# Moving the memory keys, the transposes and half of the memory values in a two-layer decoder trunk

## The chip, the cores and the metric

The kernel runs on one core of one Trainium2 chip. The metric is device time in microseconds (us) of one execution. The engines are named as in the profile: PE is TensorE's matmul, PEld its weight load, DVE is VectorE, ACT is ScalarE, POOL is GpSimd and SP is SyncE, which only issues transfers here.

## The reference

Two layers work on x of 512 tokens by 1024 channels, all in fp32. Each layer has three sub-layers, each followed by LayerNorm(alpha * x + f(x)):

```python
h = hybrid_mixer(x, ...)                 # three mixers, gated and merged, then  merged @ w_out
x = layer_norm(ALPHA * x + h, ln1_g, ln1_b)
x = layer_norm(ALPHA * x + memory_cross_attention(x, mem, xq, xkv, xo), ln2_g, ln2_b)
x = layer_norm(ALPHA * x + swiglu(x, w_up, w_down), ln3_g, ln3_b)

def memory_cross_attention(x, mem, wq, wkv, wo):   # 4 heads of 256, 256 memory tokens
    q = x @ wq;  k, v = split(mem @ wkv, 2)
    p = softmax(q k^T / 16)                        # per head
    return (p @ v) @ wo
```

The memory tokens are the same for both layers. Keys and values depend on them and on the layer's weights alone, so they can be computed at any place ahead of their use; the queries need the rows that the first LayerNorm has finished.

## The kernel before

Each fp32 operand is held as two parts: a high part, rounded to fp32r (the name ends in h), and a low part, the difference (l). A product is three matmuls: high by high, high by low, low by high. Weights come in 372 chunks of 128 x 1024. A chunk is loaded by `load_raw` (L269, on SP's queue), its high part is cast on ACT in `split_chunk` (L277), and its low part is a subtraction issued by `flush` (L284), on DVE, but on POOL for the chunks in `on_pool`: the memory key tiles 2 to 7 and the first two up-projection tile pairs. Chunks are split in the order of their use. Each step has a limit `pairs` on the chunks that are split and not yet used up; `refill` brings at most two new ones per step, and three raw chunks are loaded beyond those split. All buffers of 4 KB a partition (raw and split chunks, activations in transposed form, memory keys and values, query and output parts) come from one pool of 39, tag `a4`.

The order of the work is written out by hand in `make_program` as a list of steps for PE. Step kinds are "a" (an output tile of 128 channels by all tokens, 24 matmuls of 512 columns; for memory keys 256 columns, L828 to L830), "b" (a row tile of 128 tokens by 512 channels, 24 matmuls, L859 to L861) and "k" (all four row tiles of the cross-attention's output projection, for one head's part of the sum, L841 to L843). For each step the main loop calls `refill`, then the `post` function of the step before (the copy out of PSUM), then advances the side work, emits the matmuls, and calls `flush`. Side work is a list of Python generators: the stages of attention heads (`attn_x`, `attn_xv`), LayerNorm rows (`ln_item`) and others. Each `yield` ends a stage; a generator goes on one stage at a step, provided the steps since the last time add up to more than 0.75 (a full tile counts 1, a memory key tile 0.5). Half of the active generators go on ahead of the step's matmuls, the others in their middle. Where a step needs a result that isn't issued yet (`need`), the side work is advanced until it is.

Around the change, each layer goes: merge of the third branch, memory key tiles 0 and 1, output projection `w_out` as row tiles (first half of the channels, four row tiles; then the second half), memory key tiles 2 to 7, the memory values as four row tiles, eight query tiles, four "k" steps of `xo` (first half of the channels), four row tiles of `xo` (second half), and the FFN. `post_ln` adds a row tile to the residual (L697) and takes statistics (L698). After the second half of a row it starts `ln_item`, which normalises the row with two passes on DVE (L496, L499) and a power on POOL between them (L492), then waits some stages (3 for the first LayerNorm), and transposes the row on PE (L512), with copies to high parts on ACT (L518) and low parts on DVE (L519).

For a head of the cross-attention, `attn_x` has three stages for each of four row blocks: scores and exponentials (L444 to L450), scaling by the sum (L453, L454), transposes and split (L458 to L464). With the last block done, `attn_xv` multiplies with the values (L476 to L478) and splits the result (L479, L480) for the "k" step of that head.

Of the kernel before, what the change touches and what calls it, by code (L numbers as in the profile page):

```python
# [56 lines left out]
def make_program():  # L57

    chunks, steps = [], []

    def ch(name, l, k0, nk, c0, nc_):
        chunks.append((name, l, k0, nk, c0, nc_))
        return len(chunks) - 1

    def tile_step(name, l, c0, act, post, n0=0, n1=S, **kw):
        c = ch(name, l, 0, KT, c0, P)
        st = Step("a", [c], act=act, post=post, nk=KT, ncol=P, off=0, n0=n0, n1=n1, **kw)  # L70
        steps.append(st)
        return st

    def group(name, l, k0, nk, c0, act, post, pairs, tokens=NT, needs=None, pre=None):
        cs = [ch(name, l, k0 + 2 * k, 2, c0, 512) for k in range(nk // 2)]
        for t in range(tokens):
            st = Step("b", cs, act=act, post=post + (t,), t=t, pairs=pairs)
            if needs:
                st.need = tuple(n.format(t=t) for n in needs)
            if pre and t == 0:  # L80
                st.pre = pre
            steps.append(st)

    for l in range(L):
        def a_head(h, pairs):
            tile_step("w_in", l, OFF_AQ + P * h, "x", ("rope", l, "A", h, 0), pairs=pairs)
            tile_step("w_in", l, OFF_AK + P * h, "x", ("rope", l, "A", h, 1), pairs=pairs)

        def c_pair(u):
            tile_step("w_in", l, OFF_CQ + P * u, "x", ("rope", l, "C", u, 0))  # L90
            tile_step("w_in", l, OFF_CK + P * u, "x", ("rope", l, "C", u, 1))

        def gates(br, *ns):
            for n in ns:
                tile_step("w_in", l, OFF_GL + {"A": 0, "B": D, "C": 2 * D}[br] + P * n, "x",
                          ("gate", l, br, n))

        def project(br, n):
            c = ch({"A": "w_br_a", "C": "w_br_c"}[br], l, 0, 4, P * n, 2 * P)
            for m in (0, 1):  # L100
                steps.append(Step("a", [c], act="o" + br, post=("merge", l, br, n + m), nk=4,
                                  ncol=2 * P, off=P * m, n0=0, n1=S, need=("o%s%d" % (br, l),)))

        if l == 0:
            a_head(0, 6)
            a_head(1, 6)
            group("w_in", l, 0, KT, OFF_AV, "x", ("v", l, "A"), 6)
            gates("A", 0, 1)
            a_head(2, 4)
            gates("A", 2, 3, 4)  # L110
            a_head(3, 4)
            gates("A", 5, 6, 7)
        else:
            group("w_in", l, 0, KT, OFF_AV, "x", ("v", l, "A"), 6,
                  needs=("x%d_3_{t}" % (l - 1),), pre=("tabs",))
            for h in range(4):
                a_head(h, 5 if h < 2 else 4)
                gates("A", 2 * h, 2 * h + 1)
        group("w_in", l, 0, KT, OFF_CV, "x", ("v", l, "C"), 5)
        c_pair(0)  # L120
        gates("C", 0)
        c_pair(1)
        project("A", 0)
        project("A", 2)
        c_pair(2)
        project("A", 4)
        project("A", 6)
        c_pair(3)
        for n in range(KT):
            st = tile_step("w_in", l, OFF_RX + P * n, "x", ("rx", l, n))  # L130
            if n < 2:
                st.pre = ("gw", l, n)
            tile_step("w_in", l, OFF_RG + P * n, "x", ("rg", l, n))
            if n < KT - 1:
                gates("C", n + 1)
            if n in (3, 4, 5, 7):
                project("C", {3: 0, 4: 2, 5: 4, 7: 6}[n])
        for n in range(KT):
            tile_step("w_in", l, OFF_GL + D + P * n, "x", ("gate", l, "B", n))
        for n in range(KT):  # L140
            tile_step("w_br_b", l, P * n, "oB", ("merge", l, "B", n), need=("oB%d" % l,),
                      pre=("mem", l) if n == 5 else None)
        for kt in range(2):
            tile_step("xkv", l, P * kt, "mem", ("memk", l, kt), n0=0, n1=MEM, pairs=5)
        for h in range(2):
            group("w_out", l, 0, KT, 512 * h, "m", ("ln", l, 1, h), 5,
                  needs=("m%d" % l,))
        for kt in range(2, KT):
            tile_step("xkv", l, P * kt, "mem", ("memk", l, kt), n0=0, n1=MEM, pairs=5)
        for h in range(2):  # L150
            group("xkv", l, 0, KT, D + 512 * h, "mem", ("memv", l, h), 5, tokens=2)
        for kt in range(KT):
            tile_step("xq", l, P * kt, "x", ("xq", l, kt),
                      need=tuple("x%d_1_%d" % (l, t) for t in range(NT)))
        for h in range(4):
            steps.append(Step("k", [ch("xo", l, 2 * h, 2, 0, 512)], act="ox", k0=2 * h,
                              post=("lns", l, 2, 0) if h == 3 else None, pairs=4,
                              need=("ox%d_%d" % (l, h),)))
        group("xo", l, 0, KT, 512, "ox", ("ln", l, 2, 1), 6)
        for gi, (j0, nj) in enumerate(GROUPS):  # L160
            if gi == 0:
                cs = [ch("w_up", l, 0, KT, HID * (i % 2) + P * (i // 2), P) for i in range(4)]
                for hf in range(2):
                    for i in range(4):
                        steps.append(Step(
                            "a", [cs[i]], act="x", nk=KT, ncol=P, off=0,
                            n0=256 * hf, n1=256 * hf + 256, bank="up%d" % i,
                            post=("up", l, i // 2, i % 2) if hf else None, pairs=6,
                            need=("x%d_2_%d" % (l, 2 * hf), "x%d_2_%d" % (l, 2 * hf + 1))))
            for j in range(j0 + (2 if gi == 0 else 0), j0 + nj):  # L170
                tile_step("w_up", l, P * j, "x", ("up", l, j, 0), pairs=6)
                tile_step("w_up", l, HID + P * j, "x", ("up", l, j, 1), pairs=6)
            for h in range(2):
                group("w_down", l, j0, nj, 512 * h, "h",
                      ("ln", l, 3, h) if gi else ("acc", l, h), 7)
    return chunks, steps
# [3 lines left out]
def kernel(  # L180
# [72 lines left out]
    for s, st in enumerate(steps):  # L253
        for c in st.chunks:
            last_use[c] = s
            if first_use[c] is None:
                first_use[c] = s
    on_pool = {c for c, (name, l, k0, nk, c0, n) in enumerate(chunks)
               if (name == "xkv" and 2 * P <= c0 < D) or (name == "w_up" and c0 % HID < 2 * P)}
    raws, hi, lo, late = {}, {}, {}, []  # L260
    ptr = {"raw": 0, "split": 0}
    RAW_AHEAD = 3
# [9 lines left out]
    def split_chunk(s):  # L272
        c = ptr["split"]
        while ptr["raw"] <= c:
            load_raw()
        h, lw, raw = a4("whi", [1024], F32R), a4("wlo", [1024], F32R), raws.pop(c)
        A.copy(h, raw)  # L277
        hi[c], lo[c] = h, lw
        late.append((lw, raw, h, G if c in on_pool else V))
        ptr["split"] += 1  # L280

    def flush():
        for lw, raw, h, eng in late:
            eng.tensor_tensor(lw, raw, f(h), ALU.subtract)  # L284
        late.clear()
        while ptr["raw"] < min(NCH, ptr["split"] + RAW_AHEAD):
            load_raw()
# [20 lines left out]
    for l in range(L):  # L308
        goals["oA%d" % l] = goals["oC%d" % l] = 16
        goals["oB%d" % l] = KT  # L310
        goals["m%d" % l] = KT

    def met(k):
        return done.get(k, 0) >= goals.get(k, 1)
# [152 lines left out]

    def attn_xv(l, h, w):
        wh, wl = w
        acts["ox"].append((a4("oxh", [2, S], F32R), a4("oxl", [2, S], F32R)))  # L470
        oh, ol = acts["ox"][h]
        for k in range(2):
# [6 lines left out]
            A.copy(oh[:, k, :], o)  # L479
            V.tensor_tensor(ol[:, k, :], o, f(oh[:, k, :]), ALU.subtract)  # L480
        mark("ox%d_%d" % (l, h))
        return
        yield

    lnst, lnp = {}, {}

    def ln_item(l, which, t, waits):
# [14 lines left out]
                nc.sync.dma_start(out[t * P:(t + 1) * P, c], xt[:, c])  # L502
        if last:
            return
        for _ in range(waits):
            yield
        if t == 0:
# [182 lines left out]
    def post_ln(ps, l, which, half, t):  # L690
# [6 lines left out]
        V.scalar_tensor_tensor(xs, ps, co, xs, ALU.mult, ALU.add)  # L697
        V.bn_stats(lnst[t][:, 6 * half:6 * half + 6], xs)  # L698
        if half == 1:
            waits = 3 if which == 1 else 2 if t == NT - 1 else 1  # L700
            g = ln_item(l, which, t, waits)
            if step_side(g):
                fresh.append(g)
# [23 lines left out]
    def post_memv(ps, l, half, t):  # L727
        if half == 0 and t == 0:
            acts["mv"] = [(a4("mvh", [1024], F32R), a4("mvl", [1024], F32R)) for _ in range(2)]
        dh, dl = (m[:, 512 * half:512 * half + 512] for m in acts["mv"][t])  # L730
        A.copy(dh, ps)
        V.tensor_tensor(dl, ps, f(dh), ALU.subtract)

    def post_xq(ps, l, kt):
        h = kt // 2
# [348 lines left out]
```

## Time and profile before

| | us |
|---|---|
| median of 3 runs | 2190.14 |
| lowest, highest | 2189.81, 2190.46 |
| the profiled execution | 2190.57 |
| its span, first to last instruction | 2188.5 |

The span is what the trace covers; the execution's time has some 2 us around it. Busy time of an engine is the union of its instructions' durations; an instruction of PE is shown until its modelled end, so that neighbours overlap. In a timeline the columns are start, duration (both us), engine, line, operation, output and inputs by the program's names, shapes and a count of merged instructions; in brackets the idle time of the engine just before and what ended it. The granted clock is the share of TensorE's full speed that was allowed.

### The profile page before, as it was taken

Reading aid. Unit: us, or ns where it says so; the run is one execution under the profiler, and the core shown is the slowest. Engines: PE = TensorE matmul, PEld = TensorE weight load, DVE = VectorE, ACT = ScalarE, POOL = GpSimd, SP = SyncE. Lnnn points to the kernel's source line nnn. Section 1 sums busy time; section 2 is a strip of 40 time slices with the busy share of each in tenths; the row PEclk is TensorE's granted clock in tenths of the full one; section 3 lists DMA queues with packets and bytes.
Section 4 is the critical chain, followed back from the end, with each engine's and each line's share of the span. In section 5 each row is a group of like instructions: output and inputs, shape, how many; then the busy total and the mean of one; then the engine's idle time right before and its main releaser. Section 6 shows DMA issues by size and latency. Waiting matters only on the chain.

```text
span 2188.5 us, 26824 instructions
## 1 busy us (share of the span) xinstructions
PE 2166.5 (99%) x10516; PEld 1804.5 (82%) x10516; DVE 1233.0 (56%) x2041; ACT 926.3 (42%) x1658; POOL 289.8 (13%) x208
## 2 busy tenths in 40 slices
PE   9999999999999999999999999999999999999998
PEld 7888888888887888888888888888888878888887
DVE  6667666745746643244557666677466566332434
ACT  5555686643333322132135556766334333221330
POOL 2213202210300300000012132022103011000000
PEclk9999999999999999999999999999999999999999
DMA  7222323334422322233232223223334223223231
GB/s 263 85 73 86 93 87 97 122 105 135 145 77 97 126 77 77 100 122 105 75 124 78 73 82 106 78 90 128 114 116 155 77 96 117 86 69 136 95 97 39
DMA packets 66861, 224.36 MB, mean 103 GB/s; under 512 B 8112, under 2 KB 10160, under 8 KB 66736
## 3 DMA queue, kind: packets, MB, share of 16 engines
q1 hardware_dynamic: 66448, 222.40, 31.1%
q8 instruction: 83, 1.36, 0.2%
q14 instruction: 42, 0.34, 0.1%
q10 hardware_dynamic: 288, 0.26, 0.0%
HBM read 212.14 MB, written 2.10 MB: 98 GB/s over the span
## 4 chain that ended last, share of the span: by engine, by line
PE 71%; issue 22%; POOL 3%; DVE 2%; DMA 1%; ACT 1%; SPq 0%; DVEq 0%; POOLq 0%; ACTq 0%
PE ps L828 17%; PE ps L829 17%; PE ps L830 17%; PE ps L860 5%; PE ps L861 5%; PE ps L859 5%; POOL wlo L284 2%; PE o L429 1%; PE tp L423 1%; PE sc L356 1%; PE sc L355 1%; POOL ln L492 1%; PE o L385 1%; DMA raw<-in_wts_dram 1%; DVE x L499 1%
## 5 line engine op out<-in xcount | busy, mean ns | idle before, releaser
L828 PE MATMUL ps<-xh,whi 128*128 128x512 f32 (+1 forms) x1760 | 679.2, 386 | 0.1
L830 PE MATMUL ps<-xh,wlo 128*128 128x512 f32 (+1 forms) x1760 | 672.4, 382 | 1.3 <-POOL wlo L284 1.3
L829 PE MATMUL ps<-xl,whi 128*128 128x512 f32 (+1 forms) x1760 | 672.7, 382 | 0.2
L284 DVE TENSOR_TENSOR wlo<-raw,whi 128x1024 fp32r<-128x1024 f32 x348 | 434.6, 1263 | 47.2 <-ACT whi L277 39.7
L277 ACT CAST whi<-raw 128x1024 fp32r<-128x1024 f32 x368 | 378.9, 1045 | 150.2 <-PE ps L860 96.7
L830 PEld LDWEIGHTS ps<-xh,wlo 128*128 128x128 f32 x1760 | 330.9, 188 | 67.3 <-POOL wlo L284 2.1
L828 PEld LDWEIGHTS ps<-xh,whi 128*128 128x128 f32 x1760 | 331.1, 188 | 61.8 <-ACT xh L518 0.5
L829 PEld LDWEIGHTS ps<-xl,whi 128*128 128x128 f32 x1760 | 331.2, 188 | 60.9 <-DVE xl L519 0.5
L492 POOL TENSOR_TENSOR ln<-ln,expo 128x1 f32<-128x1 f32 x24 | 33.9, 1411 | 1180.5 <-DVE ln L491 1180.5
L859 PE MATMUL ps<-whi,hh 128*128 128x512 f32 x352 | 137.1, 390 | 0.0
L861 PE MATMUL ps<-whi,hl 128*128 128x512 f32 x352 | 137.0, 389 | 0.0
L860 PE MATMUL ps<-wlo,hh 128*128 128x512 f32 x352 | 136.9, 389 | 0.0
L761 ACT CAST hh<-fg 128x512 fp32r<-128x512 f32 x44 | 27.3, 620 | 191.8 <-DVE fg L760 191.8
L518 ACT CAST xh<-tp 128x256 fp32r<-128x256 f32 x80 | 28.0, 376 | 178.4 <-PE tp L512 101.2
L750 DVE SCALAR_TENSOR_TENSOR fg<-fg,ps 128x512 f32<-128x512 f32 x44 | 30.2, 687 | 116.9 <-ACT fg L749 116.9
L760 DVE TENSOR_TENSOR fg<-fg,ps 128x512 f32<-128x512 f32 x44 | 30.2, 687 | 114.4 <-PE ps L830 114.4
L749 ACT ACTIVATE fg<-ps 128x512 f32<-128x512 f32 x44 | 26.3, 598 | 135.1 <-PE ps L830 135.1
L697 DVE SCALAR_TENSOR_TENSOR x<-ps,x 128x512 f32<-128x512 f32 x48 | 32.9, 686 | 82.5 <-PE ps L861 82.4
L861 PEld LDWEIGHTS ps<-whi,hl 128*128 128x128 f32 x352 | 66.1, 188 | 13.8
L860 PEld LDWEIGHTS ps<-wlo,hh 128*128 128x128 f32 x352 | 66.1, 188 | 13.7
L859 PEld LDWEIGHTS ps<-whi,hh 128*128 128x128 f32 x352 | 66.1, 188 | 13.6
L859 PE MATMUL ps<-whi,mh 128*128 128x512 f32 x192 | 74.9, 390 | 0.0
(239 smaller groups left out, 3518.4 us busy)
## 6 DMA issues: line engine op xcount, KB each, us to landing
raw<-in_wts_dram SPq DMA_DIRECT2D x368, 512.0 KB, 3.6
xs<-xs SPq DMA_DIRECT2D x32, 128.0 KB, 2.2
lng<-in_lnp_in_dram SPq DMA_DIRECT2D x6, 512.0 KB, 5.1
lnb<-in_lnp_in_dram SPq DMA_DIRECT2D x6, 512.0 KB, 5.8
tabs<-in_tabs_in_dram SPq DMA_DIRECT2D x4, 512.0 KB, 7.4
x<-in_x_in_dram SPq DMA_DIRECT2D x4, 512.0 KB, 9.4
qkA<-qkA SPq DMA_DIRECT2D x16, 128.0 KB, 2.2
qkC<-qkC SPq DMA_DIRECT2D x16, 128.0 KB, 2.2
```

The lines of the kernel that those rows point to most:

```text
L277: A.copy(h, raw)
L284: eng.tensor_tensor(lw, raw, f(h), ALU.subtract)
L492: G.tensor_tensor(st[:, 15:16], st[:, 14:15], expo, ALU.pow)
L697: V.scalar_tensor_tensor(xs, ps, co, xs, ALU.mult, ALU.add)
L750: V.scalar_tensor_tensor(g, g, 1.0, ps, ALU.add, ALU.mult)
L760: V.tensor_tensor(g, g, ps, ALU.mult)
L828: T.matmul(pv, wh, xh, start=(kt == 0), stop=False)
L829: T.matmul(pv, wh, xl, start=False, stop=False)
L830: T.matmul(pv, wl, xh, start=False, stop=(kt == st.nk - 1))
L859: T.matmul(ps, xh, wh, start=(i == 0), stop=False)
L860: T.matmul(ps, xh, wl, start=False, stop=False)
L861: T.matmul(ps, xl, wh, start=False, stop=(i == n - 1))
```

## The change

It does six things. The memory key tiles 2 to 7 move between the row tiles of the second half of `w_out`: one behind the first row tile, two behind the second, one behind the third, two behind the fourth. All transposes of the first LayerNorm wait until the last row tile is through (`rows`), and then come after 0, 1, 2 and 2 more stages. The second half of the memory values (used by heads 2 and 3) moves behind the queries, and `attn_xv` waits for the half that it uses (`mv`). The limits `pairs` rise: 5 to 7 at the memory keys, 5 to 6 and 7 at `w_out`, 5 to 6 at the values, 4 to 6 and 6 to 8 at `xo`. No chunk's subtraction is on POOL any more.

```diff
-    def group(name, l, k0, nk, c0, act, post, pairs, tokens=NT, needs=None, pre=None):
+    def group(name, l, k0, nk, c0, act, post, pairs, tokens=NT, needs=None, pre=None, between=None):
         cs = [ch(name, l, k0 + 2 * k, 2, c0, 512) for k in range(nk // 2)]
...
             steps.append(st)
+            if between:
+                between[t]()
...
-        for kt in range(2):
-            tile_step("xkv", l, P * kt, "mem", ("memk", l, kt), n0=0, n1=MEM, pairs=5)
-        for h in range(2):
-            group("w_out", l, 0, KT, 512 * h, "m", ("ln", l, 1, h), 5,
-                  needs=("m%d" % l,))
-        for kt in range(2, KT):
-            tile_step("xkv", l, P * kt, "mem", ("memk", l, kt), n0=0, n1=MEM, pairs=5)
-        for h in range(2):
-            group("xkv", l, 0, KT, D + 512 * h, "mem", ("memv", l, h), 5, tokens=2)
+        def memk(*kts):
+            for kt in kts:
+                tile_step("xkv", l, P * kt, "mem", ("memk", l, kt), n0=0, n1=MEM, pairs=7)
+
+        memk(0, 1)
+        group("w_out", l, 0, KT, 0, "m", ("ln", l, 1, 0), 6, needs=("m%d" % l,))
+        group("w_out", l, 0, KT, 512, "m", ("ln", l, 1, 1), 7, needs=("m%d" % l,),
+              between=(lambda: memk(2), lambda: memk(3, 4), lambda: memk(5), lambda: memk(6, 7)))
+        def memv(h):
+            group("xkv", l, 0, KT, D + 512 * h, "mem", ("memv", l, h), 6, tokens=2)
+
+        memv(0)
         for kt in range(KT):
             tile_step("xq", l, P * kt, "x", ("xq", l, kt),
                       need=tuple("x%d_1_%d" % (l, t) for t in range(NT)))
+        memv(1)
         for h in range(4):
             steps.append(Step("k", [ch("xo", l, 2 * h, 2, 0, 512)], act="ox", k0=2 * h,
-                              post=("lns", l, 2, 0) if h == 3 else None, pairs=4,
+                              post=("lns", l, 2, 0) if h == 3 else None, pairs=6,
                               need=("ox%d_%d" % (l, h),)))
-        group("xo", l, 0, KT, 512, "ox", ("ln", l, 2, 1), 6)
+        group("xo", l, 0, KT, 512, "ox", ("ln", l, 2, 1), 8)
...
-    on_pool = {c for c, (name, l, k0, nk, c0, n) in enumerate(chunks)
-               if (name == "xkv" and 2 * P <= c0 < D) or (name == "w_up" and c0 % HID < 2 * P)}
...
-        late.append((lw, raw, h, G if c in on_pool else V))
+        late.append((lw, raw, h))
...
-        for lw, raw, h, eng in late:
-            eng.tensor_tensor(lw, raw, f(h), ALU.subtract)
+        for lw, raw, h in late:
+            V.tensor_tensor(lw, raw, f(h), ALU.subtract)
...
+        goals["mv%d_0" % l] = goals["mv%d_1" % l] = 2
...
     def attn_xv(l, h, w):
         wh, wl = w
+        while not met("mv%d_%d" % (l, h // 2)):
+            yield
...
         if last:
             return
+        if which == 1:
+            while not met("rows%d" % l):
+                yield
+            waits = min(t, 2)
         for _ in range(waits):
             yield
...
-            waits = 3 if which == 1 else 2 if t == NT - 1 else 1
+            waits = 2 if t == NT - 1 else 1
+            if which == 1 and t == NT - 1:
+                mark("rows%d" % l)
             g = ln_item(l, which, t, waits)
...
         V.tensor_tensor(dl, ps, f(dh), ALU.subtract)
+        mark("mv%d_%d" % (l, half))
```

## Rows read from the trace of the kernel before

**Rows 1.** Page, part 1: busy us (share of the span) and instructions per engine.
```profile
PE 2166.5 (99%) x10516; PEld 1804.5 (82%) x10516; DVE 1233.0 (56%) x2041; ACT 926.3 (42%) x1658; POOL 289.8 (13%) x208
```
**Rows 2.** Waits of PE over the whole span: us in total, times, longest.
```profile
PE ps L830 <- POOL wlo L284: 5.0, 6, 1.9
PE tp L512 <- DVE x L499: 3.1, 2, 1.5
```
**Rows 3.** Timeline of PE, layer 0, from the last projection row to the queries.
```profile
563.50 0.39 PE L861 MATMUL ps<-whi,ml 128*128 128x512 f32 x1
563.73 1.04 PE L512 MATMUL tp<-ident,x 128*128 128x128 f32 x8
564.52 0.36 PE L828 MATMUL ps<-mh,whi 128*128 128x256 f32 x1
...
567.59 0.28 PE L829 MATMUL ps<-ml,whi 128*128 128x256 f32 x1
569.75 0.39 PE L830 MATMUL ps<-mh,wlo 128*128 128x256 f32 x1 [1.88 <-POOL wlo L284]
...
608.41 0.39 PE L828 MATMUL ps<-xh,whi 128*128 128x512 f32 x1
```
**Rows 4.** Timelines of POOL, DVE and PE, layer 0, around the second LayerNorm.
```profile
711.86 5.72 POOL L284 TENSOR_TENSOR wlo<-raw,whi 128x1024 fp32r<-128x1024 f32 x2
711.93 3.39 DVE L499 SCALAR_TENSOR_TENSOR x<-x,ln,lnb 128x1024 f32<-128x1024 f32 x1 [0.45 <-POOL ln L492]
715.38 1.09 PE L512 MATMUL tp<-ident,x 128*128 128x128 f32 x8 [1.54 <-DVE x L499]
...
735.61 0.39 PE L830 MATMUL ps<-xh,wlo 128*128 128x256 f32 x1 [0.43 <-POOL wlo L284]
```
**Rows 5.** Timeline of DVE: chunk subtractions, one row's normalisation, the last low part.
```profile
698.22 2.35 DVE L284 TENSOR_TENSOR wlo<-raw,whi 128x1024 fp32r<-128x1024 f32 x2
...
722.70 0.68 DVE L697 SCALAR_TENSOR_TENSOR x<-ps,x 128x512 f32<-128x512 f32 x1
...
726.17 1.28 DVE L499 SCALAR_TENSOR_TENSOR x<-x,ln,lnb 128x1024 f32<-128x1024 f32 x1 [0.44 <-POOL ln L492]
...
729.42 0.42 DVE L519 TENSOR_TENSOR xl<-tp,xh 128x256 fp32r<-128x256 f32 x1 [0.44 <-ACT xh L518]
```
**Rows 6.** Windows, layer 1: stretch, length, engines' busy us, granted clock, DMA share, GB/s.
```profile
1657.50:1661.00 3.50, 3.50 (x19) 3.50 (x19) 1.79 (x5) 2.31 (x5) 2.79 (x2) 0.51 0.50 150
```
**Rows 7.** Timeline of PE, layer 0, in the four "k" steps of the cross-attention's output.
```profile
673.38 1.03 PE L458 MATMUL tp<-ident,pr 128*128 128x128 f32 x8
674.68 0.39 PE L444 MATMUL sc<-mkh,xqh 128*128 128x256 f32 x1 [0.27 <-DVE wl L464]
...
686.30 0.39 PE L843 MATMUL ps<-whi,oxl 128*128 128x512 f32 x1
...
687.75 0.39 PE L841 MATMUL ps<-whi,oxh 128*128 128x512 f32 x1
...
691.87 1.03 PE L458 MATMUL tp<-ident,pr 128*128 128x128 f32 x8
693.54 0.49 PE L476 MATMUL o<-wh,mvh 128*128 128x512 f32 x1 [0.64 <-ACT wh L463]
...
694.73 0.40 PE L476 MATMUL o<-wh,mvh 128*128 128x512 f32 x1
```
**Rows 8.** Timelines of ACT and DVE: a chunk's cast, a result's copy and subtraction.
```profile
646.35 1.04 ACT L277 CAST whi<-raw 128x1024 fp32r<-128x1024 f32 x1
647.98 0.59 ACT L741 CAST xqh<-ps 128x512 fp32r<-128x512 f32 x1 [0.60 <-PE ps L830]
648.60 0.69 DVE L742 TENSOR_TENSOR xql<-ps,xqh 128x512 fp32r<-128x512 f32 x1 [1.62 <-ACT xqh L741]
```
**Rows 9.** Windows, layer 0, second LayerNorm: PE, PEld, DVE, ACT, POOL busy, as above.
```profile
703.00:729.00 26.00, 24.46 (x121) 20.21 (x119) 20.38 (x30) 2.42 (x7) 10.22 (x5) 1.00 0.23 71
```
**Rows 10.** Page, part 6, DMA issues: count, KB each, median us from issue to landing.
```profile
raw<-in_wts_dram SPq DMA_DIRECT2D x368, 512.0 KB, 3.6
```

More of the change, by code (lines that the diff above doesn't have):

```diff
@@ L481, in attn_xv @@
         mark("ox%d_%d" % (l, h))
-        return
-        yield
     lnst, lnp = {}, {}
```

## Prediction

> **What bounds the kernel now.** I read the page's busy times first: TensorE (PE) is busy for 99% of the span [rows 1]. That figure is an upper bound of its use, because matmuls overlap: a 128x512 matmul is shown with 0.39 us, but the next one starts 0.23 us later, and 128x256 ones follow each other in 0.12 us (25 steps from 564.52 to 567.59), eight transposes take 0.79 (563.73 to 564.52) [rows 3]. So I count what is lost as the distance between starts beyond these steps; an idle gap costs 0.16 us more than the gap shown (0.39 - 0.23), or as much less as the row's own duration is shorter. Second, the table of waits says who PE waits for at all: 5.0 us for low-part subtractions on GpSimd (POOL) in 6 waits, 3.1 us for the normalised rows in 2 [rows 2]. All of these lie between the output projection and the first FFN tiles, the stretch that the change rearranges. Third, the timeline of that stretch in layer 0, whose waits come back in layer 1. No other engine is near full there over the whole stretch, so the gain is what PE loses in it, less what the new order loses.
>
> **What the change removes, per layer.**
> Key tiles: the second memory key tile behind the projection waits for its low part on POOL; 567.59 to 569.75 is 2.16 us where 0.12 is usual, 2.04 lost [rows 3]. The change does these subtractions on VectorE (DVE), 1.2 us each (2.35 for two) instead of 2.9 (5.72 for two) [rows 4, 5], and with up to 7 chunks in work they are issued one or two steps ahead. I take the whole 2.0 as gone.
> In layer 1 the granted clock fell to 0.51 for 3.5 us just behind this wait, with PE at the lower of its two levels (1.2 instead of 2.4 GHz) [rows 6]: about 1.7 us once. In layer 0 the same wait had no such drop, so I take it as gone with 0.8: 1.4 us, once.
> LN2: a POOL subtraction starts at 711.86 and the second step of the first row's normalisation on DVE (L499) at 711.93 takes 3.39 us instead of 1.28 [rows 4, 5]; the transposes behind it leave PE idle for 1.54 us, 1.7 with the matmul's overlap. Without POOL's work L499 ends at 713.2, before PE's last matmul of the row (its wait began near 713.8): 1.7 gone. Two of the first up-projection tiles wait for POOL (0.43 idle [rows 4] and 0.2, the rest of 2.5 us a layer [rows 2]; 0.59 and 0.36 lost); the change issues those chunks at the second xo row tile already (limit 8 instead of 6), three steps earlier: 0.95 gone.
> Cross-attention's end: head 3's whole chain runs inside the four xo steps. Transposes to scores 673.38 to 674.68 is 1.30 where eight transposes take 0.79 [rows 3, 7]: 0.5. xo head 2 waits for its operand: 686.30 to 687.75 is 1.45 for four steps of 0.23: 0.54. Head 3's transposes to its value matmuls: 1.67 against 0.79, 0.88, and 1.19 for the next three against 0.68, 0.5. xo head 3 waits as head 2 did, 0.54 [rows 7]. Together 3.0. With the two memory value tiles behind the queries (2 x 24 x 0.227 = 10.9 us) each phase of heads 2 and 3 comes two steps earlier against xo: value matmuls of head 2 at xo step 0, head 3's transposes at step 1, its values at step 2, so each result is 5.4 us old when needed. All 3.0 gone.
> Sum removed: 2.0 + 1.7 + 0.95 + 3.0 = 7.7 per layer.
>
> **What it adds, per layer.** The matmuls are the same in number and shape. The costs come from cover that got shorter.
> LN1: before, 44.7 us lay between the last projection row and the first query matmul (563.73 to 608.41) [rows 3]. Now the cover is 2 key tiles, 2 value tiles and 4 rows of transposes: 2 x 24 x 0.12 + 2 x 24 x 0.227 + 4 x 0.79 = 19.8 us. All transposes are held until the last row tile is through, and then come at T = 0 (row 0), 6.6 (row 1), 12.9 (row 2) and 16.5 (row 3, in the middle of the second value tile). Behind them DVE is one in-order queue, in program order: row 3's normalisation to T = 5.0 (0.2 to start, 4.75 from 722.70 to 727.45 [rows 5]); row 0's four low parts, 2.4 as they take turns with ScalarE (ACT), to 7.4; two chunk subtractions 2.35 to 9.7; key tile 0.4; two more chunks to 12.4; key tile to 12.8; row 1 to 15.2; two chunks to 17.5; a value tile 0.7 to 18.2 [rows 8]; row 2 to 20.6; row 3's first pair at 21.1, its last at 23. PE asks for row 3's first pair at 19.8 (high part) and 20.0 (low part); later pairs are used only every 1.4 us. So the first query tile loses 0.9 to 1.1 us: I take 1.0. From below: 0, if DVE is 1.3 us quicker than this chain; from above 3.3, if two more subtractions (2.35) stand in front. 1.0 is the chain's own sum. The fourth value chunk's low part comes at 11.3 and is asked for at 11.8: free, with 0.5 of margin.
> Holding the transposes costs nothing of itself: rows 0 to 2 are normalised long before, and the key tiles that stand between the row tiles give DVE 8.4 us (a row and one key tile) for a row's 4.75 and 1 to 2 subtractions.
> Values moved: head 2's value matmuls now come right behind the second moved tile and read its result. Copy (0.59) and subtraction (0.69) follow the last matmul's end [rows 8]; three matmuls on the older tile cover 0.7. Two chunk casts at 1.04 each stand in front on ACT, behind the softmax of head 3, and end about 0.4 late. I take 0.9; 0.2 without the casts, 2.0 if the subtractions behind them are in the way too.
> LN2: DVE takes two subtractions (2.35) between row 0 and row 1 of the normalisation, while PE is 1.7 earlier than before. Counted from the start of the xo row tiles (5.45 us each), row 0 ends at 5.65 + 4.75 = 10.4, row 1 at 10.4 + 2.35 + 4.75 = 17.5, row 2, behind row 0's low parts, at 17.5 + 2.4 + 4.75 = 24.6; PE asks for them at 10.9, 10.9 + 0.8 + 5.45 = 17.2, and 17.5 + 0.1 + 0.8 + 5.45 = 23.8. Lost: 0.3 + 0.8 and 0.1 for a restart: 1.2; 0 if the queue keeps up, 2.4 if all of it is paid.
> Earlier chunks: SyncE's queue issues each raw load behind the previous one, when one of the 39 buffers comes free. I count 35 in use at the row tiles, 37 to 39 at the value tiles (memory stays alive until behind the queries) and 37 at LN2. The projection's 8 input tiles and 8 weight tiles come free just at T = 0, and the loads needed next take those. No wait of PE leads to a raw load now, so nothing can be gained here, and I take nothing lost; a rival below takes the opposite. Moved steps issue no DMA of their own beside these loads; POOL keeps only its 1.5 us powers here, and DVE pays 10 x 1.2 = 12 us more per layer, of which 1.0 + 1.2 reach PE.
> Sum added: 1.0 + 0.9 + 1.2 = 3.1 per layer.
>
> **The sum.** 2 x (7.7 - 3.1) + 1.4 = 10.6 us. The profiled execution took 2190.57 (span 2188.5 and 2.1 around it): 2180.0. The median shown is 0.4 below it: 2179.5.
>
> **The rivals.**
> DVE is given too much: in the stretch around LN2 it is busy 20.4 of 26 us [rows 9] and near full, since a queue that waits for ACT's copies between its own pieces can't fill the rest. If the upper ends hold (3.3, 2.0, 2.4), 7.7 per layer comes back: 2 x 0 + 1.4, 2188.7, no change that can be told. Against it: 2.1 of the 20.4 are the stretch of L499, which goes.
> The Trainium skill (Perfetto Trace Analysis, "Optimizing Scalar/DVE Operations") says that with VectorE saturated it may help to hand work to GpSimd, the opposite of this edit, though it adds that the two share a read port and this might not help; this trace bears out the caveat: L499 with a POOL subtraction beside it took 3.39 us, without 1.28.
> Buffers run out (the slower side): if the load of a query chunk gets a buffer only when a subtraction of T = 12.4 is done, it lands 3.6 later [rows 10], the second near 17, its cast ends at 18, and the copies of rows 1 to 3, behind it in ACT's order, come 6.3 late: 7.3 instead of 1.0 lost at LN1. The same at LN2's first up tiles costs 1 more. 2 x 7.3 - 10.6 = +4.0: 2194.1 by the median, and 2 us more for each us that the buffer comes later. It bites as soon as a load waits beyond T = 7 or 8, as the casts would then pass 12.1, and outweighs the gain from about 10.4 on. Against it: the free buffers counted above.
> DVE keeps up and nothing is given back: 2 x 7.7 + 1.7 = 17.1, 2173.0.
> The layer 1 clock drop stays, or moves behind another wait: 1.4 less gain, 2180.9, inside the forecast's own range.
>
> **How the numbers follow.** Forecast 0.62 (own range 2175 to 2184.5), nothing given back 0.18, DVE overloaded 0.13, buffers 0.07. A difference under 0.2%, 4.4 us, can't be told from no change. Faster by that: 0.62 + 0.18 and a little of the third, 0.82; same 0.12, most of the third; slower 0.06, the buffer case, which at its price stands at the edge and is told apart if the buffer comes any later. The range leaves out the buffer case and the edges: 2172.5 to 2187.5.
>
> **What would show it.** Right: no wait for a POOL subtraction; L499 at 1.3 us in all rows; xo steps without a wait for ox; a wait of the first query tile for x near 1 us and shorter ones of LN2's transposes for L499. Wrong: a gap of several us ahead of the queries, with DVE busy through it (overloaded) or ACT waiting for a raw load (buffers); PE waiting for mv by more than 2 us at xo's start; or the time unchanged although these waits went.

## The result, and the profile after

The changed kernel takes 2177.69 us (median of 4 runs, 2177.11 to 2178.37) against 2189.97 (2188.81 to 2190.46) for the kernel before, ratio 0.9945 with a 95% interval of 0.9928 to 0.9962. Its profiled execution took 2178.37 with a span of 2176.5; forecast were 2179.5, between 2172.5 and 2187.5.

The first view to compare is the page's busy time. It answers to [rows 1], and shows what not to read the gain from: PE is busy 2.8 us less in a span that is 12 us shorter, and still 99%.

```profile
PE 2163.7 (99%) x10516; PEld 1803.7 (83%) x10516; DVE 1236.4 (57%) x2061; ACT 927.2 (43%) x1658; POOL 236.9 (11%) x188
```

DVE has the 20 subtractions more that POOL has less, some 23 us, and is busy only 3.4 us longer; most of the difference lies in the passes of L499, eight of which took 3.4 us beside POOL's work before and none does now (48.5 us in sum before, 31.7 after). The second view is the table of waits of PE over the whole span (us in total, times, longest). The waits for POOL of [rows 2] are gone, the one for normalised rows is a third, and a wait for a value tile is new.

```profile
PE warm L880 <- DVE zero L877: 1.4, 1, 1.4
PE tp L521 <- DVE x L504: 1.0, 2, 0.5
PE ot L401 <- DVE st L376: 1.0, 1, 1.0
PE ps L924 <- ACT xh L905: 0.8, 1, 0.8
PE o L483 <- ACT mvh L742: 0.5, 2, 0.2
```

I added up, matmul by matmul, how far each start lies beyond the usual step (0.227 us behind 512 columns, 0.12 behind 256, 0.098 behind the 128 of a transpose, as in [rows 3]). Between the row tiles of the projection and the first up tiles that was 10.0 us in layer 0 and 11.5 in layer 1 before, and is 4.2 and 4.2 after: 13.1 less. The spans differ by 12.0; the missing 1.1 lies at the program's start, where the same sum is 1.1 higher in the first 40 us: from 5.5 to 10.5 us PE ran 10 matmuls where it had run 19 before, in the same busy time, and the first record of a granted clock lies at 10.5 us instead of 5.5. In another execution of the changed kernel (the run of it among the experiments) that record lies at 5.3 us, PE runs 21 matmuls in the same 5 us, and the start costs 0.3 less than before. So the 1.1 belongs to the one execution, and the gain is all in the stretch that was rearranged.

Of the 4.2 that are left per layer, half lies in three places; the rest are restarts of 0.1 to 0.3 us, which the kernel before has too. First the timeline of PE at the end of the first LayerNorm, layer 0. Row 0's transposes start at 576.41 (T = 0 of the prediction), row 3's at 593.01, and the first query tile at 596.64; its second matmul should start at 596.87 and waits until 597.01 for a low part.

```profile
576.41 1.04 PE L521 MATMUL tp<-ident,x 128*128 128x128 f32 x8
...
593.01 1.03 PE L521 MATMUL tp<-ident,x 128*128 128x128 f32 x8
...
596.64 0.39 PE L840 MATMUL ps<-xh,whi 128*128 128x512 f32 x1
597.01 0.50 PE L841 MATMUL ps<-xl,whi 128*128 128x512 f32 x1
597.35 0.39 PE L842 MATMUL ps<-xh,wlo 128*128 128x512 f32 x1
```

DVE's timeline beside it shows the queue of the prediction: row 3's normalisation ends at 581.39 (T = 5.0), row 0's low parts follow, then chunks and rows in turn.

```profile
580.10 1.29 DVE L504 SCALAR_TENSOR_TENSOR x<-x,ln,lnb 128x1024 f32<-128x1024 f32 x1 [0.44 <-POOL ln L497]
581.30 0.42 DVE L528 TENSOR_TENSOR xl<-tp,xh 128x256 fp32r<-128x256 f32 x1
...
583.70 2.35 DVE L288 TENSOR_TENSOR wlo<-raw,whi 128x1024 fp32r<-128x1024 f32 x2
...
596.21 0.76 DVE L528 TENSOR_TENSOR xl<-tp,xh 128x256 fp32r<-128x256 f32 x2 [0.44 <-ACT xh L527]
```

Second, the timeline of PE where head 2 reads the moved value tile (L483 to L485), and ACT's beside it: two chunk casts end at 671.73, and the copy of the value tile starts only as they end (671.63).

```profile
671.62 0.39 PE L485 MATMUL o<-wh,mvl 128*128 128x512 f32 x1
672.25 0.50 PE L483 MATMUL o<-wh,mvh 128*128 128x512 f32 x1 [0.24 <-ACT mvh L742]
672.59 0.40 PE L484 MATMUL o<-wl,mvh 128*128 128x512 f32 x1
672.98 0.50 PE L485 MATMUL o<-wh,mvl 128*128 128x512 f32 x1
```

```profile
669.74 1.99 ACT L281 CAST whi<-raw 128x1024 fp32r<-128x1024 f32 x2
671.63 0.58 ACT L742 CAST mvh<-ps 128x512 fp32r<-128x512 f32 x1
```

Third, DVE and PE at the second LayerNorm, which answer to [rows 4]. L504 (L499 before) takes 1.28 us; row 0 is in time, and the two chunk subtractions between rows 0 and 1 make row 2's transposes late by 0.52 (with these on POOL, in the third experiment, row 2 is in time).

```profile
709.19 1.28 DVE L504 SCALAR_TENSOR_TENSOR x<-x,ln,lnb 128x1024 f32<-128x1024 f32 x1 [0.45 <-POOL ln L497]
710.40 2.35 DVE L288 TENSOR_TENSOR wlo<-raw,whi 128x1024 fp32r<-128x1024 f32 x2
...
723.22 1.28 DVE L504 SCALAR_TENSOR_TENSOR x<-x,ln,lnb 128x1024 f32<-128x1024 f32 x1 [0.44 <-POOL ln L497]
```

```profile
724.55 1.09 PE L521 MATMUL tp<-ident,x 128*128 128x128 f32 x8 [0.52 <-DVE x L504]
```

### The profile page after: what moved, and what is told of

Its sections match the earlier page's. It is cut to its first block, busy times and chain, and to the rows that moved or that the text cites. A ratio compares the mean times of both kernels' runs of the same rounds, so it can differ in the third digit from the quotient of the medians.

```text
span 2176.5 us, 26775 instructions
## 1 busy us (share of the span) xinstructions
PE 2163.7 (99%) x10516; PEld 1803.7 (83%) x10516; DVE 1236.4 (57%) x2061; ACT 927.2 (43%) x1658; POOL 236.9 (11%) x188
## 4 chain that ended last, share of the span: by engine, by line
PE 95%; DVE 2%; ACT 1%; issue 0%; POOL 0%; DMA 0%; DVEq 0%; ACTq 0%
PE ps L841 21%; PE ps L840 21%; PE ps L842 21%; PE ps L871 7%; PE ps L872 7%; PE ps L873 7%; PE o L434 1%; PE tp L428 1%; PE sc L361 1%; PE sc L360 1%; PE o L390 1%; PE ps L854 1%; PE ps L855 1%; PE ps L853 1%; PE tp L521 1%
## 5 line engine op out<-in xcount | busy, mean ns | idle before, releaser
L288 DVE TENSOR_TENSOR wlo<-raw,whi 128x1024 fp32r<-128x1024 f32 x368 | 456.1, 1256 | 46.6 <-ACT whi L281 39.1
```

Of the source, the lines that this page charges most:

```text
L288: V.tensor_tensor(lw, raw, f(h), ALU.subtract)
```

## The experiments

Eleven runs in three sets; within a set the kernels ran on the same chip, with the kernel before beside them (median 2191.37, 2191.26 and 2190.52). Each has the median of its runs and the ratio to the kernel before with its interval. "Lost per layer" is the sum of starts beyond the usual step, as above, in layer 0.

**All subtractions on DVE, nothing else.** `late.append((lw, raw, h, V))` in the kernel before.

> The kernel before with one edit: all low-part subtractions on DVE, order and limits untouched. Theory A (the move from POOL pays only because the chunks are also split earlier): behind the last row tile DVE has row 3's normalisation (5.0 us) and row 0's low parts (2.4) in front of the low part of memory key tile 3, which PE asks for about 4 us after the row tile; it waits some 4.6 us instead of 2.0. At LN2, L499 falls to 1.3 us and 1.7 us are won, but up tile 2 waits about 1.9 for its low part instead of 0.95 in two waits. Per layer 2.6 lost, 0.7 won: 2190 + 3.8 = about 2194, up to 2197 if the clock falls behind the longer waits. Theory B (the subtractions on POOL were the cost, by themselves): 2.0 + 1.7 + 0.95 per layer and the clock drop go: about 2179.

2202.16 us, 1.0053 [1.0041, 1.0066]: slower by 10.8, theory A's direction and more than its size; theory B fell. The timelines of DVE and PE, layer 0, show the predicted wait in its predicted length (4.4 idle, 4.56 lost): the key chunk's subtraction, the first of the two at 570.97, stands behind row 3's normalisation and row 0's low parts.

```profile
567.37 1.28 DVE L499 SCALAR_TENSOR_TENSOR x<-x,ln,lnb 128x1024 f32<-128x1024 f32 x1 [0.44 <-POOL ln L492]
568.57 0.42 DVE L519 TENSOR_TENSOR xl<-tp,xh 128x256 fp32r<-128x256 f32 x1
...
570.97 2.35 DVE L284 TENSOR_TENSOR wlo<-raw,whi 128x1024 fp32r<-128x1024 f32 x2
```

```profile
572.24 0.58 PE L830 MATMUL ps<-mh,wlo 128*128 128x256 f32 x1 [4.40 <-DVE wlo L284]
572.62 0.42 PE L828 MATMUL ps<-mh,whi 128*128 128x256 f32 x1
...
741.66 0.39 PE L830 MATMUL ps<-xh,wlo 128*128 128x256 f32 x1 [3.52 <-DVE wlo L284]
```

Two things were larger: the wait of up tile 2 (3.5 instead of 1.9 us, as the chain of rows in front of it on DVE was later against PE than I had reckoned), and the clock behind both waits (last section). Lost per layer: 17.1 instead of 10.0.

**The limits of before in the changed kernel.** 7 to 5 at the keys, 6 and 7 to 5 at `w_out`, 6 to 5 at the values, 6 to 4 and 8 to 6 at `xo`.

> The changed kernel with the limits on split chunks as before (5 at the keys, projection and values, 4 and 6 at xo). Theory A: key tile 4 is split only at its own step, behind row 1's normalisation on DVE, and key tile 7 behind row 3's: waits of about 2.8 and 4.7 us for L288, and about 1 more at up tile 2: 8 us per layer lost, 2178 + 16 = about 2194, more if the clock falls. Theory B: the order alone does it and the limits add nothing: 2178 to 2180.

2211.39 us (2205.64 to 2213.43 in four runs), 1.0087 [1.0074, 1.0101]. The waits came where theory A put them, 2.9 idle at key tile 4 and 4.4 at key tile 7, and 3.5 at up tile 2 where 1 was expected; the rest of the 34 us goes with the clock, which was granted at 0.51 behind them (from 587.8 to 594.7, for one). PE's timeline, layer 0:

```profile
563.09 0.39 PE L842 MATMUL ps<-mh,wlo 128*128 128x256 f32 x1 [2.90 <-DVE wlo L288]
...
589.71 0.58 PE L842 MATMUL ps<-mh,wlo 128*128 128x256 f32 x1 [4.41 <-DVE wlo L288]
...
746.49 0.58 PE L842 MATMUL ps<-xh,wlo 128*128 128x256 f32 x1 [3.52 <-DVE wlo L288]
```

**POOL's subtractions back in the changed kernel.** `on_pool` and its use as before.

> The changed kernel with the subtractions of key tiles 2 to 7 and of the first four up tiles on POOL again. Theory A: with the chunks split earlier these are done before PE asks, so only the stretched L499 of row 0 at LN2 comes back (1.7 us), while rows 1 and 2 no longer wait there (1.1): 0.6 per layer, 2179 to 2180. Theory B: POOL's slower subtractions cost what they did (2.0 + 1.7 + 0.95 per layer): 2187.

2179.29 us, 0.9946 [0.9932, 0.9959], as theory A had it: with the chunks split early, POOL's slow subtractions cost little, 0.8 per layer by the trace (5.0 lost). Only the stretched pass of row 0 at LN2 reaches PE again, with the same wait as before (DVE's timeline, then PE's table of waits for the whole span).

```profile
708.40 3.40 DVE L506 SCALAR_TENSOR_TENSOR x<-x,ln,lnb 128x1024 f32<-128x1024 f32 x1 [0.44 <-POOL ln L499]
```

```profile
PE tp L523 <- DVE x L506: 3.1, 2, 1.5
```

**The values alone.** The kernel before, with `memv` for the second half behind the queries and the wait for it in `attn_xv`.

> The kernel before with one edit: the second half of the memory values behind the queries, with the wait for it, limits untouched. Theory A: the waits in the xo steps (3.0 us per layer) go, 0.8 comes back where head 2's values read the tile just made: 2.2 per layer, about 2185.6. Theory B: the gain of that move needs the higher limits at xo (chunks late at the xo steps, PE waiting for L284 there): under 1 us per layer, 2188 to 2190.

2185.40 us, 0.9973 [0.9963, 0.9984]: theory A. Lost per layer are 7.9, 2.1 less: the waits in the xo steps are gone at the old limits too, and the one for the value tile has come (0.5 in 2 waits). The wait of 1.9 for the key tile stays, and with it the clock's drop in layer 1 (0.50 granted from 1655.9 to 1659.3).

**DVE and limits, without the moves.** The kernel before with all subtractions on DVE and the limits raised as in the change.

> The kernel before with two edits: all subtractions on DVE and the higher limits; keys, transposes and values where they were. Theory A (these two belong together and make up most of the gain; the values make up the rest; the keys' place none): the xo steps keep their waits of 3.0 us per layer, the rest is as in the changed kernel with the keys back: 4.4 us above that one, 2180.5 to 2181.5. Theory B: without the moved values the chunks at the xo steps stand in front of the heads on DVE and more is lost: 2184 or above.

2180.48 us, 0.9956 [0.9943, 0.9969]: theory A. Lost per layer 5.9, of which 3.0 in the xo steps; PE's table of waits has them as before ([rows 7]) and none for a key or up chunk (L860 is a row tile, outside the stretch):

```profile
PE warm L868 <- DVE zero L865: 1.4, 1, 1.4
PE o L476 <- ACT wh L463: 1.3, 2, 0.6
PE ot L396 <- DVE st L371: 1.0, 1, 1.0
PE tp L512 <- DVE x L499: 1.0, 2, 0.5
PE sc L444 <- DVE wl L464: 0.5, 2, 0.3
PE ps L860 <- DVE wlo L284: 0.3, 1, 0.3
```

**The keys behind the projection again, transposes not held.** In the changed kernel:

```diff
-              between=(lambda: memk(2), lambda: memk(3, 4), lambda: memk(5), lambda: memk(6, 7)))
+              )
+        memk(2, 3, 4, 5, 6, 7)
...
-        if which == 1:
-            while not met("rows%d" % l):
-                yield
-            waits = min(t, 2)
...
+            waits = 3 if which == 1 else 2 if t == NT - 1 else 1
```

> The changed kernel with the key tiles 2 to 7 behind the projection again and the transposes of the first LayerNorm not held (3 stages as before); limits, DVE subtractions and moved values stay. Theory A: with limit 7 the key chunks are split ahead of the row tiles' end, so their place brings nothing by itself, and the longer cover takes away the 0.26 us per layer that the first query tile waits: 2177 to 2178. Theory B: the place between the row tiles is what hides the key chunks' subtractions: 2 us or more per layer come back, 2182 or above.

2175.98 us, 0.9932 [0.9918, 0.9946]. Theory B fell: the place between the row tiles hides nothing that the limits don't.

**The keys back, the transposes still held** (the first hunk alone), and **the changed kernel again** on the same chip.

> The changed kernel with the key tiles behind the projection again, the transposes still held (which does little, as the rows are through by then). It parts the two edits undone together before. Theory A: the longer cover alone takes away the first query tile's 0.26 us per layer, and with the keys there holding or not makes no difference: 0.3 to 0.9 us under the changed kernel on this chip, as with both undone. Theory B: it is the earlier transposes that made that kernel faster: this one equals the changed kernel.

> The changed kernel itself, on the same chip as the three beside it, so that differences under 2 us can be read. Both theories: 2177 to 2179; 0.9945 of the kernel before, as first timed.

2176.01 us, 0.9936 [0.9923, 0.9949], and 2176.93, 0.9939 [0.9926, 0.9952]. The runs of the two overlap (2175.39 to 2177.16, 2176.32 to 2177.47), so by time alone the keys' place is not told from nothing. By the trace they lose 3.7 and 4.2 per layer. Holding or not makes no difference with the keys there.

**Not held, keys between** (the other hunks alone).

> The changed kernel with the transposes of the first LayerNorm not held (3 stages, as before); the key tiles stay between the row tiles. Row 0's transposes then come at key tile 5, while the projection's 8 input tiles are still in use. Theory A: the 8 new input tiles don't fit beside them in the 39 buffers, so ACT's copies wait for the last row tile's end with the casts of value chunks behind them: 1 to 3 us per layer, 2180 to 2184. Theory B: holding is needless, DVE's queue at the tail gets shorter and the first query tile's wait (0.26) goes: 2177.

2180.46 us, 0.9951 [0.9939, 0.9964]. The size was theory A's and the mechanism was not. Row 0's transposes start at 566.85, and ACT copies the first pair of tiles at once (567.48). The other three copies wait for DVE, whose low part of the first stands behind a row's normalisation, and not for buffers: all are made by 573.8, with the last row tile still to come (DVE takes that one up at 576.53). PE's timeline and ACT's show what costs instead. A value chunk is late by 0.39, and row 3's transposes, three stages behind its normalisation, stand right ahead of the first query tile, which waits for their copies; two casts and a value copy are in front of these on ACT.

```profile
584.87 0.50 PE L866 MATMUL ps<-wlo,mh 128*128 128x512 f32 x1 [0.39 <-DVE wlo L288]
...
595.31 0.93 PE L517 MATMUL tp<-ident,x 128*128 128x128 f32 x7
596.39 0.51 PE L834 MATMUL ps<-xh,whi 128*128 128x512 f32 x1 [0.16 <-ACT xh L523]
597.17 0.50 PE L835 MATMUL ps<-xl,whi 128*128 128x512 f32 x1 [0.28 <-DVE xl L524]
```

```profile
567.48 0.37 ACT L523 CAST xh<-tp 128x256 fp32r<-128x256 f32 x1 [5.21 <-PE tp L517]
572.18 0.65 ACT L523 CAST xh<-tp 128x256 fp32r<-128x256 f32 x2 [4.33 <-DVE xl L524]
...
593.59 2.00 ACT L281 CAST whi<-raw 128x1024 fp32r<-128x1024 f32 x2
595.49 0.58 ACT L736 CAST mvh<-ps 128x512 fp32r<-128x512 f32 x1
595.96 0.38 ACT L523 CAST xh<-tp 128x256 fp32r<-128x256 f32 x1
```

Counted by the distances between starts, 0.7 more is lost at the value chunk and 0.7 at the first query tile, the whole of the 1.4 per layer by which this run (5.6) lies above the changed kernel. So holding pays through the order of the work on DVE and ACT; that row 3's transposes come a stage earlier with it is the likely reason at the query tile, which no run tests by itself.

**What is left, taken away.** In the changed kernel, at the "k" steps:

```diff
-        if side and (st.kind == "k" or st.kind == "a" and st.nk < KT):
+        if side and st.kind == "a" and st.nk < KT:
...
             for t in range(NT):
+                if side and t == 1:
+                    side()
...
-                              post=("lns", l, 2, 0) if h == 3 else None, pairs=6,
+                              post=("lns", l, 2, 0) if h == 3 else None, pairs=8,
```

> The changed kernel, and two additions: in the xo steps the side work comes after the first of four row tiles instead of ahead of all, and the limit at these steps is 8 instead of 6. Theory A: head 2's value matmuls no longer stand right behind the value tile that they read (0.8 us per layer), and the two up chunks are split before row 0 of LN2 is due, so rows 1 and 2 are not late (1.1): 1.9 per layer, 2177.7 - 3.8 = about 2174. Theory B: the copies of head 3's result are late for the last xo step, or the transposes lack PSUM banks beside the four open ones: 2177 to 2179.

2174.10 us, 0.9923 [0.9910, 0.9935]: theory A. PE's table of waits has neither the value tile nor the normalised rows any more, and 2.5 us per layer are lost instead of 4.2. The two additions ran together; which of them took which wait away is read from the waits. The last run joins it with the keys back and the transposes not held:

> Both improvements together: key tiles 2 to 7 behind the projection and transposes not held, side work in the middle of the xo steps, limit 8 there. Theory A (the losses are separate): 0.3 us per layer less than with the middle side work alone, about 2173.4, and 1.3 to 1.8 us per layer under the changed kernel. Theory B (the earlier chunks at the xo steps and the longer cover take the same DVE time): no better than 2174.1.

2173.10 us (2172.60 to 2173.93), 0.9922 [0.9908, 0.9936], with 2.0 lost per layer: 3.8 us under the changed kernel beside it, and the runs of the two don't overlap. Whether the keys' place adds to the side work's 2174.1 can't be told. Its table of waits, whole span, holds nothing of the stretch:

```profile
PE warm L877 <- DVE zero L874: 1.4, 1, 1.4
PE ot L402 <- DVE st L377: 1.0, 1, 1.0
PE ps L869 <- DVE wlo L289: 1.0, 1, 1.0
PE ps L921 <- ACT xh L902: 0.5, 1, 0.5
PE ps L922 <- DVE xl L903: 0.2, 1, 0.2
```

## Why the prediction was right

It was right in direction and mechanism; the gain of 12.2 us in the profiled executions (12.3 by the medians) was forecast as 10.6. That they lie so close is in part chance: the stretch itself gained 13.1, 2.5 more than forecast, and the slower start of the one profiled execution hid 1.1 of it. Step by step, per layer:

- What goes (7.7): all four terms went in full. The clock drop in layer 1 went too (1.5 by the sums of the two layers; 1.4 was counted).
- LN1's shorter cover (1.0 forecast): 0.26 lost. This is the mis-sized term. The chain was read rightly, but neighbouring instructions of DVE overlap by some 0.08 us in the trace, so that row 3's first low part came at T = 20.5, not 21.1, and restarts behind the transposes moved PE's demand from 19.8 to 20.2.
- The moved values (0.9): 672.25 to 673.32 and the gap before them lose 0.40 + 0.11 + 0.16 + 0.11 = 0.79, with ACT's two casts in front as told.
- LN2 (1.2): 0.20 + 0.11 for row 1 and 0.68 + 0.11 for row 2, 1.1.
- The sum: 7.7 - 2.15 = 5.55 forecast by these sizes, 5.8 counted (10.0 to 4.2), twice, and 1.5 for the clock: 13.1, of which 1.1 was lost at the start.

Of the rivals, the overloaded DVE, the missing buffers and the clock drop behind another wait did not come. "DVE keeps up" didn't either: LN2's two waits show that it did not everywhere.

One reading was incomplete. The prediction booked the waits for POOL under the move to DVE with the earlier split as its helper. The runs turn this round: earlier splits with POOL reach 2179.3, DVE with the old limits 2202.2 without the other moves, 2211.4 with them. The limits are what pays at the key and up tiles; on top of them DVE gives the LN2 pass back, 0.8 per layer by the trace (5.0 to 4.2 lost), too little to be told by the ratios (0.9946 against 0.9945 and 0.9939). The higher limits alone, with the old order and POOL's subtractions, are in no run, so what they bring without the other edits is not shown. The values are worth 2.1 per layer alone, by the trace, and 4.5 us on top of the others on one chip (2180.5 to 2176.0). The keys' move gives nothing (by the trace it costs 0.5 per layer) and rests on holding the transposes. My count of the 39 buffers was too high as well: it had 35 in use at the row tiles, which leaves 4, and the run without the hold filled 8 new input tiles there.

## What to carry to other kernels

Before a helper's work is moved to another engine, list what stands ahead of it in that engine's order at the step that needs it: the same subtraction, of key tile 3, was free when the higher limits let it end at 553.8 us, and cost 4.4 us when it stood behind a row's normalisation and ended at 572.2. With an engine that is 99% busy, count the distance between starts; the waits lay in a sixth of the program, and the sum over its rows forecast the gain to 1.6 us, 2.5 in the stretch itself. A result that is read right behind the step that makes it costs its copies; a quarter of a step of other work between them (one row tile of four) took that away.

## What the runs showed of the hardware

A DVE pass with a POOL subtraction beside it was longer by what was left of POOL's instruction: 3.39 in [rows 4], 3.40 with POOL back, 1.28 to 1.29 in every run without. The Trainium skill (SBUF — State Buffer, "Who interferes with whom") says that a VectorE instruction with two inputs in SBUF, as L499 has, contends with a GpSimd instruction that reads SBUF, and calls the shared port pair an exclusive lock. The rows agree: POOL's subtractions take 2.39 at the median, so the one that starts at 711.86 ends near 714.25, and 1.28 later is 715.5, against 715.3 measured.

The clock was not expected to cost as much. Behind waits of 3.5 and 4.4 us PE went on at the lower level (1.2 GHz) for 3.5 to 6.9 us, though not behind each of them. The windows of the kernel with DVE alone (layer 0 behind each of its two waits, layer 1 behind the first; the columns are those of [rows 6]):

```profile
571.70:575.20 3.50, 2.96 (x14) 2.96 (x15) 3.50 (x5) 2.95 (x4) 0.00 (x0) 0.51 0.49 142
742.30:745.80 3.50, 3.50 (x19) 3.50 (x19) 2.71 (x3) 0.00 (x0) 0.00 (x0) 0.51 0.41 149
1663.90:1670.80 6.90, 4.50 (x21) 4.50 (x22) 5.65 (x8) 4.43 (x6) 0.00 (x0) 0.51 0.25 79
```

While PE is busy there it does half its work: 1.5, 1.7 and 2.2 us lost besides the waits. Behind the second wait of layer 1, 3.5 us again, there is no such stretch. In the kernel before, the same wait of 1.88 us was followed by such a stretch in layer 1 and not in layer 0; in the changed kernel, whose longest wait in the stretch is 0.5 us, the granted clock stays at 1.00 from its first record, at 10.5 us, to behind the last matmuls, at 2171 us.
